# Expert weights of a mixture-of-experts block in twelve 16 KB slots, one 2 MB load each, and no normed copy of the tokens

## The chip, the cores and the metric

The kernel runs on one core of one Trainium2 chip. The metric is the device time in microseconds (us), the median of several runs. All data are float32 in HBM. On the chip, SBUF has 128 partitions; sizes of tiles below are bytes per partition.

## The reference, cut to what matters

256 tokens of width 1024 go through two transformer blocks. Block 1 and the front of block 2 (mixers, attention, a cross attention to a memory) are dense. Behind them stand 16 experts, of which each takes the 32 tokens that score highest for it:

```python
def ec_moe(h, router_w, w_gu, w_down):          # h = rmsnorm(x) * g
    cap = 2 * n // 16                           # 32
    aff = softmax(einsum('bnd,de->bne', h, router_w))
    gates, idx = top_k(swapaxes(aff, 1, 2), cap)
    xs = h[idx]
    def expert(xe, wgu, wd):                    # wgu 1024 x 4096, wd 2048 x 1024
        ga, up = split(xe @ wgu, 2)
        return (silu(ga) * up) @ wd
    ys = map(expert, (xs, w_gu, w_down)) * gates
    return zeros(n, d).at[idx].add(ys)
...
x = x + ec_moe(...)
return rmsnorm(x, final_norm_g)
```

One expert's weights are 16 MB (gate and up) and 8 MB (down); all of them are 384 MB, each byte read once and used for 32 tokens.

## The kernel before

One class, `Body`, writes the program; `run` (L213) calls `block1_mix`, `block1_ffn`, `block2_mix`, `cross` and `moe` one after the other. All loads are issued by the sync engine's queue (SP), in program order: a load that waits for its place holds up those behind it.

**Dense part.** A weight unit of 1 MB is loaded into one of three `raw` buffers (L49, L55), and `split` (L59) turns it into an exact sum of two float32r tiles, `wh` by ScalarE (L67) and `wl` by VectorE (L68). Both come from the ring `hl` of eight 8 KB buffers, so four units are split at a time. `mm3` (L81) multiplies in three passes: H with H, L with H, H with L. `raw` and `hl` lie in one pool, `big`.

**End of the dense part.** `proj_out` with `w_out_2` (L714) multiplies the mixers' output `yH`, `yL` (tiles of the pool `m2`) with four split units. `cross` (L984) then projects queries with two split units of `ca_wq`, from the tokens `xh`, `xl` (pool `xt`, 16 KB), attends to keys and values `mK`, `mV` (pool `mkv`, 8 KB; last read on L1019), and multiplies with `ca_wo` as it is, from two `raw` buffers (L1031). Its small tiles `q`, `qT`, `aE`, `apT` are in the pool `caw`. `route` (L1035) makes the router's logits from `xf`, the transposed tokens (L1054), and has GpSimd write `h`, the tokens times their 1/rms (L1055).

**Experts.** `moe` (L1057) finds each expert's 32 tokens as a one-hot matrix `OH` (L1116). For four experts at a time `gather` (L1126) multiplies `h` with `OH` into `xs`. For each expert (L1119), eight blocks k of 128 rows are loaded in two halves, `eload(wgu[...])` (L1148), each 128 rows of 8 KB, and multiplied on four column groups of TensorE at once (L1150). Then Silu (L1164), times U (L1165), four transposes (L1169), a copy `aT` (L1171), eight `down` loads with their matmuls (L1179), a copy `ys` of each half of the columns (L1190 by ScalarE, L1192 by VectorE, both into one tile), and a matmul that scatters it to the tokens (L1194). The last expert's down weights come in pieces of columns (L1229), so that the end of the work is small; behind that stand the final norm and the store (L1248).

**Slots.** A load goes to the next of 21 slots of 8 KB (L1067 to L1070), in the order in which they fall free: nine pools `e0` to `e8`, opened from the right end of SBUF downwards, the eight `hl` buffers, the three `raw` buffers and `xf`. A pool that lies over older tiles waits for those it overlaps:

```python
e_ = [(self.open("e%d" % i, 1, es, "right"), "e", 1) for i in range(9)]
raw, hl = (self.big, "raw", self.NR), (self.big, "hl", self.NH)
slots = (e_[3:6] + [hl] * 4 + [raw] + [hl] * 4 + e_[:3] + e_[6:8] + [raw] * 2 + e_[8:] + [(ep, "xf", 1)])
```

`eload` (L1077) keeps the loads in their order. On the right side lie, from the end downwards, `xt` (16 KB), `mkv` (8 KB), `m2` (49 KB, whose lowest 16 KB are `yH` and `yL`), and below it tiles of the mixers that are done earlier.

Of the kernel before, what the change touches and what calls it, by code (L numbers as in the profile page):

```python
# [26 lines left out]
class Body:  # L27
# [10 lines left out]
    def psum_pool(self, **banks):  # L38
        """the 8 banks of PSUM, dealt out anew"""
# [7 lines left out]
    def unit(self, w, u, c0):  # L47
        """rows 512 u .. 512 u + 511, 512 columns from c0"""
        raw = self.big.tile([128, 4, 512], F32, name="raw", tag="raw", bufs=self.NR)  # L49
        self.nc.sync.dma_start(raw, w.rearrange("(u k p) c -> u p k c", p=128, k=4)[u][:, :, c0:c0 + 512])  # L50
        return raw

    def unit_c(self, w, c0):
        """1024 rows, 256 columns from c0"""
        raw = self.big.tile([128, 8, 256], F32, name="raw", tag="raw", bufs=self.NR)  # L55
# [15 lines left out]
    def queued(self, behind):  # L71
        """issue what follows behind the given instructions of the same engines"""
# [8 lines left out]
    def mm3(self, out, pairs, first=True, last=True):  # L81
        """pairs: ((lhsT H, lhsT L), (rhs H, rhs L)) per 128 of the contraction."""
# [6 lines left out]
    def gemm_T(self, x, ws):  # L89
        """x @ W by 128 tokens: two of [tok 128, 512]"""  # L90
# [7 lines left out]
    def gemm_t(self, x, ws, t):  # L98
        """x @ W for the tokens of half t: [tok 128, 512]"""
# [6 lines left out]
    def gemm_W(self, x, w, tag="acc"):  # L106
        """(x @ W)^T for 256 columns of W: [feature 128, 2 x 256 tok]"""
# [13 lines left out]
    def rstd(self, ss, n, scale, tag="rs", eng=None):  # L121
        """1/sqrt(ss*scale + eps) on [128, n]: a first guess from the exponent, then Newton's iteration"""
# [23 lines left out]
    def sumsq(self, src, junk):  # L146
        """sum of squares over the free axis of the given [128, n] pieces"""
# [9 lines left out]
    def norm_T(self, x, gname):  # L157
        """rmsnorm(x) * g, transposed, as exact sum H + L; the two halves of the tokens one by one"""
# [30 lines left out]
    def post_norm_a(self, t, halves, eng=None):  # L189
        """1/rms of a half of the tokens"""  # L190
# [5 lines left out]
    def post_norm_b(self, halves, g):  # L196
        """times the gain"""
# [6 lines left out]
    def post_norm_c(self, t, y, r):  # L204
        """x[:, t] += y * r"""
# [7 lines left out]
    def run(self):  # L213
# [8 lines left out]
        self.NR, self.NH = 3, 8  # L222
        self.big = self.open("big", 1)
        st = ExitStack()
# [20 lines left out]
        self.close(self.work2, mkv, self.xtp)  # L245
# [1049 lines left out]
```

## Time and profile before

| | |
|---|---|
| median of 3 runs | 1561.36 us (1559.75 to 1562.66) |
| the profiled execution, first to last instruction (span) | 1558.2 us; the median run is 3.2 us longer |
| TensorE busy | 1286.3 us (83%), mean granted clock 0.875 |
| VectorE, ScalarE, GpSimd busy | 417.2, 351.3, 42.9 us |
| read from HBM | 501.05 MB, 322 GB/s over the span |
| loads of expert weights | 376 of 1 MB; 14, 2 and 4 of 512, 256 and 128 KB at the end |

PE is TensorE's matmuls, PEld its weight loads, DVE VectorE, ACT ScalarE, POOL GpSimd; SPq is the sync engine's queue, which issues the DMAs. A float32 matmul stands in the trace as two records. Tile names lose their numbers, and the 8 KB slots are called `eraw`. PEclk is the clock granted to TensorE, as a share of 2.4 GHz. Times in the rows are us from the start of the span.

### The profile page before, as it was taken

The page shows a single profiled execution, that of the slowest core. Times are in us where ns is not written, and L with a number is a line of the kernel's source. Part 1 is how long each engine was busy: PE and PEld are TensorE (multiplying, and loading weights), DVE is VectorE, ACT ScalarE, POOL GpSimd, SP SyncE. Part 2 cuts the span into 40 slices and gives each one's busy share as a digit, 9 for nine tenths or more (in the row PEclk, how much of TensorE's full clock was granted, in tenths as well). Part 3 has the DMA queues.
Part 4 walks back from the last instruction along what each step waited for, and adds up shares of the span by engine and source line. Part 5 has one row for each costly group of instructions (what it writes and reads, how often), then busy time and mean ns, then how long its engine had stood idle before and what let it go on. Part 6 is the DMA issues. An engine that isn't in the chain of part 4 may idle for free.

```text
span 1558.2 us, 17805 instructions
## 1 busy us (share of the span) xinstructions
PE 1286.3 (83%) x7429; PEld 680.1 (44%) x7429; DVE 417.2 (27%) x753; ACT 351.3 (23%) x608; POOL 42.9 (3%) x97
## 2 busy tenths in 40 slices
PE   6999999999999998886777777768767768777676
PEld 5998988999978775321121111112111102111112
DVE  5644557544467764200000000000000000000002
ACT  5445546444356643000000000000000000000002
POOL 1100012000020001000000000000000000000000
PEclk9999999999999999897868868778779778778777
DMA  8744437555532389899999999999999999999996
GB/s 272 242 162 135 156 117 240 191 190 189 180 112 94 110 321 365 346 420 420 421 421 421 420 421 421 420 421 420 421 421 421 420 421 420 421 420 421 421 420 244
DMA packets 137360, 503.26 MB, mean 323 GB/s; under 512 B 14251, under 2 KB 68287, under 8 KB 89152
## 3 DMA queue, kind: packets, MB, share of 16 engines
q1 hardware_dynamic: 137280, 502.13, 82.0%
q8 instruction: 58, 0.95, 0.3%
q14 instruction: 22, 0.18, 0.0%
HBM read 501.05 MB, written 1.05 MB: 322 GB/s over the span
## 4 chain that ended last, share of the span: by engine, by line
DMA 56%; PE 11%; DVE 1%; ACT 1%; issue 0%; SPq 0%; DVEq 0%; ACTq 0%
DMA eraw<-in_expert_w_gu_dram 37%; DMA eraw<-in_expert_w_down_dram 19%; PE acc L86 4%; PE sm L1150 1%; PE acc L1031 1%; PE sm L86 1%; PE sm L1179 1%; PE po L955 0%; PE sm L1132 0%; PE at L947 0%; PE sm L765 0%; PE sm L870 0%; PE po L1019 0%; PE at L978 0%; PE sm L1012 0%
## 5 line engine op out<-in xcount | busy, mean ns | idle before, releaser
L1150 PE MATMUL sm<-eraw,xs 128*32 128x512 f32 x2048 | 366.4, 811 | 168.4 <-DMA eraw<-in_expert_w_gu_dram 168.4
L1179 PE MATMUL sm<-eraw,aT 128*32 128x512 f32 (+2 forms) x1088 | 227.0, 672 | 42.0 <-DMA eraw<-in_expert_w_down_dram 30.6
L1150 PEld LDWEIGHTS sm<-eraw,xs 128*32 128x32 f32 x2048 | 48.9, 123 | 459.5 <-DMA eraw<-in_expert_w_gu_dram 423.1
L68 DVE TENSOR_TENSOR wl<-raw,wh 128x1024 fp32r<-128x1024 f32 x166 | 197.8, 1220 | 101.1 <-ACT wh L67 100.8
L67 ACT ACTIVATE wh<-raw 128x1024 fp32r<-128x1024 f32 x166 | 168.1, 1054 | 154.2 <-PE sm L86 67.7
L1165 DVE TENSOR_TENSOR es<-es,sm 128x512 f32<-128x512 f32 x16 | 11.0, 687 | 570.0 <-PE sm L1150 564.0
L1179 PEld LDWEIGHTS sm<-eraw,aT 128*32 128x32 f32 x1088 | 53.6, 121 | 201.4 <-DMA eraw<-in_expert_w_down_dram 93.0
L1164 ACT ACTIVATE es<-sm 128x512 f32<-128x512 f32 x16 | 9.6, 597 | 444.9 <-PE sm L1150 444.8
L1192 DVE COPY ys<-sm 128x512 f32<-128x512 f32 (+2 forms) x18 | 11.3, 632 | 235.5 <-PE sm L1179 235.5
L1190 ACT ACTIVATE ys<-sm 128x512 f32<-128x512 f32 x16 | 9.6, 597 | 252.3 <-PE sm L1179 252.3
L1194 PE MATMUL acc<-ys,ogT 128*128 128x512 f32 (+2 forms) x136 | 59.8, 581 | 1.3 <-ACT ys L1190 0.8
L86 PE MATMUL acc<-xh,wl 128*128 128x256 f32 x352 | 51.6, 284 | 0.0
L86 PE MATMUL acc<-xl,wh 128*128 128x256 f32 x352 | 50.4, 282 | 0.0
L86 PE MATMUL acc<-xh,wh 128*128 128x256 f32 x352 | 50.0, 283 | 0.0
L86 PE MATMUL sm<-xh,wh 128*128 128x256 f32 x352 | 49.6, 284 | 0.0
L86 PE MATMUL sm<-xh,wl 128*128 128x256 f32 x352 | 48.9, 281 | 0.0
L86 PE MATMUL sm<-xl,wh 128*128 128x256 f32 x352 | 48.9, 281 | 0.0
L86 PEld LDWEIGHTS sm<-xh,wh 128*128 128x128 f32 x352 | 46.1, 191 | 0.6
L86 PEld LDWEIGHTS acc<-xh,wl 128*128 128x128 f32 x352 | 45.5, 189 | 0.5
L86 PEld LDWEIGHTS acc<-xh,wh 128*128 128x128 f32 x352 | 45.0, 188 | 0.5
L86 PEld LDWEIGHTS acc<-xl,wh 128*128 128x128 f32 x352 | 45.2, 189 | 0.1
L86 PEld LDWEIGHTS sm<-xh,wl 128*128 128x128 f32 x352 | 44.9, 189 | 0.0
(381 smaller groups left out, 1337.0 us busy)
## 6 DMA issues: line engine op xcount, KB each, us to landing
eraw<-in_expert_w_gu_dram SPq DMA_DIRECT2D x256, 1024.0 KB, 19.8
eraw<-in_expert_w_down_dram SPq DMA_DIRECT2D x120, 1024.0 KB, 19.8
raw<-in_w_in_dram SPq DMA_DIRECT2D x34, 1024.0 KB, 5.2
raw<-in_w_gate_dram SPq DMA_DIRECT2D x11, 1024.0 KB, 5.2
raw<-in_w_up_dram SPq DMA_DIRECT2D x11, 1024.0 KB, 5.2
raw<-in_w_down_dram SPq DMA_DIRECT2D x11, 1024.0 KB, 4.9
raw<-in_w_out_dram SPq DMA_DIRECT2D x8, 1024.0 KB, 4.9
eraw<-in_expert_w_down_dram SPq DMA_DIRECT2D x14, 512.0 KB, 11.6
```

The source lines that it names most:

```text
L67: nc.scalar.activation(H[:, k], raw[:, k], AF.Copy)
L68: self.at["L"] = nc.vector.tensor_tensor(L[:, k], raw[:, k], H[:, k].bitcast(F32), OP.subtract).ins
L86: nc.tensor.matmul(out, l[i], r[j], start=first and p == 0 and q == 0, stop=last and p == 2 and q == n - 1)
L1031: nc.tensor.matmul(acc[c], o[:, k, t * 128:(t + 1) * 128], w[c][:, k, :], start=k == 0, stop=k == 3)
L1150: nc.tensor.matmul(dst[32 * j:32 * j + 32, :], xs[:, k, 32 * q:32 * q + 32], raw[:, 512 * j:512 * j + 512], start=k == 0, stop=k == 7, til ...
L1164: nc.scalar.activation(s, G, AF.Silu)
L1165: nc.vector.tensor_tensor(s, s, U, OP.mult)
L1179: nc.tensor.matmul(y[c0][32 * c:32 * c + 32, 0:n], aT[:, c, 32 * j:32 * j + 32], raws[hh][:, o:o + n], start=j == 0, stop=j == 3, tile_pos ...
L1190: nc.scalar.activation(ys[:, c], y[c0][:, 0:n], AF.Copy)
L1192: nc.vector.tensor_copy(ys[:, c], y[c0][:, 0:n])
L1194: nc.tensor.matmul(out[t], ogT[:, t * 128:(t + 1) * 128], ys[:, c], start=first, stop=last)
```

## The change

- The two halves of a split unit become one 16 KB tile; `hl` is a ring of four. `raw` gets a pool of its own, `rawp`, closed ahead of `moe`. `ep` is opened at the start.
- The slots are twelve of 16 KB: eight pools from the right end, and the four `hl` buffers. `raw` and `xf` are slots no more; `xf` moves to `cross`'s pool `ca`.
- One load brings 2 MB: a block of 128 whole rows of the gate and up weights (16 KB each), or 512 rows of down weights, four to a partition (16 KB in one run).
- `h` is gone: `gather` multiplies `x`. Each expert gets the 1/rms of its 32 tokens by eight matmuls of one column (`OH` with `rc`), a copy `rs`, and applies it as the scale of Silu and in the multiplication with U.
- `ys` is a tile of one half of the columns, in one buffer of 2 KB. The final norm's row, its copies and the junk tile share one slot.
- The scratch memory for descriptors of GpSimd's DMAs falls to 1 KB per partition; the kernel issues none.

```diff
-        raw = self.big.tile([128, 4, 512], F32, name="raw", tag="raw", bufs=self.NR)
+        raw = self.rawp.tile([128, 4, 512], F32, name="raw", tag="raw", bufs=self.NR)
...
-        H = self.big.tile([128, n, c], F32R, name="wh", tag="hl", bufs=self.NH)
-        L = self.big.tile([128, n, c], F32R, name="wl", tag="hl", bufs=self.NH)
+        HL = self.big.tile([128, 2, n, c], F32R, name="whl", tag="hl", bufs=self.NH)
+        H, L = HL[:, 0], HL[:, 1]
...
-        self.NR, self.NH = 3, 8
+        self.NR, self.NH = 3, 4
+        self.ep = self.open("ep", 1)
         self.big = self.open("big", 1)
+        rawst = ExitStack()
+        self.rawp = self.open("rawp", 1, rawst)
...
-        self.close(self.work2, mkv, self.xtp)
+        self.close(rawst, mkv, self.xtp)
...
-            self.h = self.sb(self.ep, [128, 2, D], "h4")
-            self.xf = self.sb(rt, [128, 8, 256], "xf", tag="xf")
+            self.xf = self.sb(ca, [128, 8, 256], "xf")
+            self.rc = self.sb(rt, [128, 2], "rc")
...
-        ss = self.sumsq([x[:, t, 0:512], x[:, t, 512:1024]], h[:, t, :])
+        ss = self.sumsq([x[:, t, 0:512], x[:, t, 512:1024]], cw.tile([128, 512], F32, name="sqj", tag="q"))
...
+        nc.gpsimd.tensor_copy(self.rc[:, t:t + 1], self.r4[t])
...
-        nc.gpsimd.tensor_scalar(h[:, t, :], x[:, t, :], self.r4[t], None, OP.mult)
...
-            e_ = [(self.open("e%d" % i, 1, es, "right"), "e", 1) for i in range(9)]
-            raw, hl = (self.big, "raw", self.NR), (self.big, "hl", self.NH)
-            slots = (e_[3:6] + [hl] * 4 + [raw] + [hl] * 4 + e_[:3] + e_[6:8] + [raw] * 2 + e_[8:] + [(ep, "xf", 1)])
+            e_ = [(self.open("e%d" % i, 1, es, "right"), "e", 1) for i in range(8)]
+            hl = (self.big, "hl", self.NH)
+            slots = e_[2:5] + [hl] * 2 + e_[:1] + [hl] * 2 + e_[1:2] + e_[5:8]
...
-                return pool.tile([128, 2048], F32, name="eraw", tag=tag, bufs=bufs)
+                return pool.tile([128, 4096], F32, name="eraw", tag=tag, bufs=bufs)
...
-                    for half, dst in ((0, G), (1, U)):
-                        raw = eload(wgu[e, 128 * k:128 * k + 128, 2048 * half:2048 * half + 2048])
+                    raw = eload(wgu[e, 128 * k:128 * k + 128, :])
+                    for o, dst in ((0, G), (2048, U)):
...
                 p = self.ps()
+                for j in range(4):
+                    for t in range(2):
+                        nc.tensor.matmul(p[32 * j:32 * j + 32, 256:257], OH[:, t, e, :], self.rc[:, t:t + 1],
+                                         start=t == 0, stop=t == 1, tile_position=(0, 32 * j))
+                rs = self.small.tile([128, 1], F32, name="rsl", tag="st9", bufs=2)
+                nc.vector.tensor_copy(rs, p[:, 256:257])
...
-                nc.scalar.activation(s, G, AF.Silu)
-                nc.vector.tensor_tensor(s, s, U, OP.mult)
+                nc.scalar.activation(s, G, AF.Silu, scale=rs)
+                nc.vector.scalar_tensor_tensor(s, U, rs, s, OP.mult, OP.mult)
...
-                def rows(j, hh):
-                    return wdn[e, 512 * j + 256 * hh:512 * j + 256 * hh + 256].rearrange("(p i) n -> p i n", i=2)
-
-                ys = ew.tile([128, D], F32, name="ys", tag="ys")
+                def rows(j):
+                    return wdn[e, 512 * j:512 * j + 512].rearrange("(p i) n -> p i n", i=4)
...
                 def scatter(c0, n, out, first, last):
-                    c = slice(c0, c0 + n)
+                    ys = ew.tile([128, n], F32, name="ys", tag="ys")
...
-                        raws = [eload(rows(j, hh).rearrange("p i n -> p (i n)")) for hh in range(2)]
+                        raw = eload(rows(j).rearrange("p i n -> p (i n)"))
...
-                        for hh in range(2):
-                            nc.sync.dma_start(raws[j][hh].rearrange("p (i n) -> p i n", i=2)[:, :, c0:c0 + m],
-                                              rows(j, hh)[:, :, c0:c0 + m])
+                        nc.sync.dma_start(raws[j].rearrange("p (i n) -> p i n", i=4)[:, :, c0:c0 + m],
+                                          rows(j)[:, :, c0:c0 + m])
...
-    nc = bacc.Bacc("TRN2", target_bir_lowering=False, num_devices=1)
+    nc = bacc.Bacc("TRN2", target_bir_lowering=False, num_devices=1, dynamic_dma_scratch_size=1024)
```

## Rows read from the trace of the kernel before

**Rows 1.** Chain that ended last, in order of time: start, us, what.
```profile
654.40 8.29 PE sm L1179 x53
662.69 20.07 DMA eraw<-in_expert_w_gu_dram
...
1534.94 9.48 DMA eraw<-in_expert_w_down_dram
```

**Rows 2.** Windows: us, busy us of each engine, PEclk, DMA share, GB/s.
```profile
100.00:200.00 100.00, 99.43 (x698) 89.83 (x697) 53.38 (x93) 54.09 (x99) 0.00 (x0) 1.00 0.46 153
...
565.50:602.50 37.00, 36.04 (x171) 26.18 (x170) 19.93 (x51) 16.06 (x40) 0.00 (x0) 1.00 1.01 413
602.50:607.50 5.00, 4.96 (x32) 3.61 (x31) 4.10 (x14) 2.68 (x7) 0.00 (x0) 1.00 0.27 102
...
626.00:633.00 7.00, 6.07 (x32) 3.20 (x32) 2.58 (x11) 0.00 (x0) 0.00 (x0) 0.61 0.10 27
...
640.00:1520.00 880.00, 655.92 (x3248) 143.29 (x3248) 34.82 (x58) 34.28 (x62) 0.00 (x0) 0.80 1.01 421
```

**Rows 3.** Waits of the SP queue, 640 to 1500: us in total, times, longest.
```profile
SPq L1080 <- DMA eraw<-in_expert_w_gu_dram: 482.5, 229, 3.4
```

**Rows 4.** DMA issues, whole span: KB each, median us from issue to landing.
```profile
eraw<-in_expert_w_gu_dram SPq DMA_DIRECT2D x256, 1024.0 KB, 19.8
```

**Rows 5.** SP queue in order of time, windows of 1 us: start, us, line, tiles.
```profile
564.79 1.55 SPq L1080 DMA_DIRECT2D eraw<-in_expert_w_gu_dram  x3
...
591.85 1.28 SPq L1080 DMA_DIRECT2D eraw<-in_expert_w_gu_dram  x3
...
606.46 0.81 SPq L1080 DMA_DIRECT2D eraw<-in_expert_w_gu_dram  x2
...
618.50 0.33 SPq L1080 DMA_DIRECT2D eraw<-in_expert_w_down_dram  x1
631.59 0.33 SPq L1080 DMA_DIRECT2D eraw<-in_expert_w_down_dram  x1
```

**Rows 6.** TensorE in order of time, 569 to 634: start, us, line, tiles.
```profile
573.77 0.39 PE L86 MATMUL sm<-wl,yH 128*128 128x512 f32 x1
...
605.27 1.16 PE L1019 MATMUL po<-apT,mV 128*128 128x128 f32 x8
...
616.46 1.96 PE L1054 MATMUL po<-rw,xf 128*128 128x16 f32 x16
...
629.60 2.82 PE L1150 MATMUL sm<-eraw,xs 128*32 128x512 f32 x16
```

**Rows 7.** DMA queue in 640:1500, 283.7:288.5, 295.4:300.4: packets, MB, share of 16 engines.
```profile
q1 hardware_dynamic: 49622, 361.34, 101.1%
...
q1 hardware_dynamic: 1040, 1.05, 64.1%
...
q1 hardware_dynamic: 272, 1.05, 60.2%
```

**Rows 8.** TensorE in order of time, one expert, idle before and its releaser in brackets.
```profile
1399.97 1.94 PE L1150 MATMUL sm<-eraw,xs 128*32 128x512 f32 x8 [1.42 <-DMA eraw<-in_expert_w_gu_dram]
...
1405.28 1.13 PE L1169 MATMUL sm<-ident,es 128*128 128x128 f32 x4 [0.88 <-DVE es L1165]
1407.15 7.50 PE L1179 MATMUL sm<-eraw,aT 128*32 128x512 f32 x32 [0.75 <-ACT aT L1171]
...
1424.22 3.70 PE L1194 MATMUL acc<-ys,ogT 128*128 128x512 f32 x8
```

**Rows 9.** Waits of TensorE and of ScalarE, 0 to 565: us in total, times, longest.
```profile
PE sm L185 <- POOL rstd L129: 10.8, 1, 10.8
...
ACT wh L67 <- PE sm L86: 67.7, 21, 8.0
```

**Rows 10.** TensorE in order of time, end of the last expert.
```profile
1523.46 1.06 PE L1150 MATMUL sm<-eraw,xs 128*32 128x512 f32 x8 [0.80 <-DMA eraw<-in_expert_w_gu_dram]
...
1543.04 2.24 PE L1179 MATMUL sm<-eraw,aT 128*32 128x256 f32 x22 [0.29 <-DMA eraw<-in_expert_w_down_dram]
1545.62 1.13 PE L1194 MATMUL acc<-ys,ogT 128*128 128x256 f32 x4 [0.34 <-DVE ys L1192]
```

More of the change, by code (lines that the diff above doesn't have):

```diff
@@ L53, in unit_c @@
     def unit_c(self, w, c0):
-        raw = self.big.tile([128, 8, 256], F32, name="raw", tag="raw", bufs=self.NR)
+        raw = self.rawp.tile([128, 8, 256], F32, name="raw", tag="raw", bufs=self.NR)
         self.nc.sync.dma_start(raw, w.rearrange("(k p) c -> p k c", p=128)[:, :, c0:c0 + 256])
@@ L506, in mem_T @@
         L = self.sb(pool, [128, 8, 256], "memL", F32R, tag=tags[1])
-        m = self.big.tile([128, 2, D], F32, name="mem", tag="raw", bufs=self.NR)
+        m = self.rawp.tile([128, 2, D], F32, name="mem", tag="raw", bufs=self.NR)
         nc.sync.dma_start(m, self.a["mem_2"][0].rearrange("(t p) d -> p t d", p=128))
@@ L550, in d_unit @@
             def d_unit(j):
-                raw = self.big.tile([128, 4, 512], F32, name="raw", tag="raw", bufs=self.NR)
+                raw = self.rawp.tile([128, 4, 512], F32, name="raw", tag="raw", bufs=self.NR)
                 nc.sync.dma_start(raw.rearrange("p (k h) c -> p k (h c)", k=2),
@@ L601, in unit_kv @@
     def unit_kv(self, u):
-        raw = self.big.tile([128, 4, 512], F32, name="raw", tag="raw", bufs=self.NR)
+        raw = self.rawp.tile([128, 4, 512], F32, name="raw", tag="raw", bufs=self.NR)
         wr = self.a["w_in_2"][0].rearrange("(u k p) c -> u p k c", p=128, k=4)[u]
@@ L699, in block2_mix @@
                 nc.scalar.activation(so[:, t, :], acc[:, 256:512], AF.Tanh, scale=0.5)
-            band = self.big.tile([128, 2, 4, 136], F32, name="band", tag="raw", bufs=self.NR)
+            band = self.rawp.tile([128, 2, 4, 136], F32, name="band", tag="raw", bufs=self.NR)
             nc.sync.dma_start(band, a["band_c"])
@@ L708, in block2_mix @@
             self.close(ms)
-            self.ep = self.open("ep", 1)
-            self.work2 = ExitStack()
-            self.work = self.open("work2", 2, self.work2)
-            self.gains = self.open("gains2", 1, self.work2)
+            work2 = ExitStack()
+            self.work = self.open("work2", 2, work2)
+            self.gains = self.open("gains2", 1, work2)
             xT, factor, scale, trans = self.norm_T(self.x, "norm_mem_g_2")
@@ L716, in block2_mix @@
             self.behind = [(), (p["h", 0], p["s", 0])]
+            self.close(work2)
         return xT
@@ L905, in attn2_rope @@
         kT = self.sb(m2, [128, 256], "kT2")
-        buf = self.big.tile([128, 2048], F32, name="rope", tag="raw", bufs=self.NR)
+        buf = self.rawp.tile([128, 2048], F32, name="rope", tag="raw", bufs=self.NR)
         ro = buf[:, 0:1280].rearrange("p (t h e) -> p t h e", t=2, h=10)
@@ L1098, in moe @@
                 nc.tensor.transpose(p[0:NE, t * 128:(t + 1) * 128], aff[:, t, :], self.ident)
-            tk = ew.tile([NE, 4, 256], F32, name="tk", tag="ys")
+            tk = ew.tile([NE, 4, 256], F32, name="tk", tag="xs")
             w1, w2, mk, po = (tk[:, i, :] for i in range(4))
@@ L1208, in moe @@
                     nc.vector.tensor_tensor(x[:, t, c], x[:, t, c], acc[2 * t + n], OP.add)
-            grow = slot()[0:1, 0:D]
+            end = slot()
+            grow, g, junk = end[0:1, 0:D], end[:, D:2 * D], end[:, 2 * D:3 * D]
             nc.sync.dma_start(grow, a["final_norm_g_2"].rearrange("(o d) -> o d", o=1))
-            g = slot()[:, 0:D]
             for n in range(2):
@@ L1215, in moe @@
                 nc.scalar.activation(g[:, 512 * n:512 * n + 512], p, AF.Copy)
-            junk, fo = slot(), slot().rearrange("p (t n) -> p t n", t=2)
+            fo = slot()[:, 0:2 * D].rearrange("p (t n) -> p t n", t=2)
             ss = self.small.tile([128, 16], F32, name="ss", tag="st1", bufs=4)
@@ L1224, in moe @@
                     if i == 0:
-                        raws[j] = [slot() for _ in range(2)]
+                        raws[j] = slot()
                     m = 512 if j < 3 else n
                     if c0 < 768 or j == 3:
-                        for hh in range(2):
-                            nc.sync.dma_start(raws[j][hh].rearrange("p (i n) -> p i n", i=2)[:, :, c0:c0 + m],
-                                              rows(j, hh)[:, :, c0:c0 + m])
+                        nc.sync.dma_start(raws[j].rearrange("p (i n) -> p i n", i=4)[:, :, c0:c0 + m],
+                                          rows(j)[:, :, c0:c0 + m])
                         if j < 3:
```

31 lines of the change are left out of this document (14 added, 17 removed).

## The prediction, made before the changed kernel was built

> **What bounds the kernel now.** I read the chain of waits first. From 662.69 us to 1544.4 us it is expert loads and, but for short pieces, nothing else; ahead of that it is mostly TensorE [rows 1]. The windows by stage say the same: in the dense part TensorE is busy 99.43 of 100 us at full clock with the DMA engines at 0.46; from 640 to 1520 us the DMA share is 1.01 at 421 GB/s, while TensorE is busy 656 of 880 us [rows 2]. So there are two regimes, and what counts is when the second begins, how fast it runs, and what follows its last byte.
>
> The waits of the SP queue say what holds a load back in the second regime: another load's landing, 482.5 us in 229 waits [rows 3]. A load takes 19.8 us to land [rows 4], and at 421 GB/s 1 MB takes 2.49 us, so eight are always under way. Slots don't limit there.
>
> They do between the regimes. The windows show the DMA engines busy from 565.5 to 602.5, at 0.27 from 602.5 to 607.5, and at 0.10 from 626 to 633 [rows 2]: 0.73 x 5 + 0.90 x 7 = 10 us idle. The first gap is a wait for a slot: three loads go at 591.85, the next at 606.46 [rows 5], behind the attention matmuls that end at 606.4 [rows 6]. In the second all 21 slots are full, and the next load, at 631.59 [rows 5], needs a slot that the first expert has used; its matmuls begin at 629.60 [rows 6], when the router is done.
>
> **The change part by part.** The sum is made against the span of 1558.2 us; the median run is 3.2 us above it.
>
> *A, room ahead of the experts.* 12 slots of 2 MB hold 24 MB, 21 of 1 MB hold 21. If all of it lands before TensorE frees a slot, 3 MB more are there when the stream restarts: 3 x 2.49 = 7.5 us. The restart itself comes later, since a slot is free only when both halves of k = 0 are used: the first 16 records end at 632.42 [rows 6], against 631.59 for the load that now needs one half [rows 5]; 0.8 us. A = -6.7.
>
> Does it all land? I place the slots by adding up the pools' sizes from both ends of SBUF. `e2` lies over mixer tiles that are done: issued at 564.8, where the first is now [rows 5]. `e3` and `e4` lie over `yL` and `yH`, last read by a matmul that starts at 573.77 and takes 0.39 [rows 6]; `w_out_2`'s two `hl` pairs fall free with them: 8 MB at about 574.2. `e0` is `xt`, free with `ca_wq`'s pairs at 591.85 [rows 5]: 6 MB. `e1` (`mkv`) and `e5` (over `aE`, `apT`) follow at 606.5, `e6` and `e7` (over `xf` and `raw`) at 618.5, when the logits' matmuls end [rows 6]. At 2.49 us per MB: 2 MB last to about 574, with a gap of some 1 us; 8 MB to 595; 6 to 610; 4 to 620; 4 to 630. The restart is at 633, so 3 us are left. Were the three last slots free 4 us later, nothing would change; were any of it wrong by more, A would fall towards -3. Bounds -7.5 and -3. Removing `h` is worth nothing: GpSimd wrote it beside other work, and `gather` waits for `OH`, not for it.
>
> *B, the size of the packets.* The stream's cost per byte may change, since each run in HBM is 16 KB and not 8. From 640 to 1500 the queue's packets took 101.1% of 16 x 860 us for 361.34 MB: 40.4 us of engine time per MB (1,048,576 bytes), in 144 packets [rows 7]. A single load of 1 KB runs took 64.1% of 16 x 4.8 = 49.2 us in 1040 packets [rows 7]. The line through both is 38.95 us plus 9.9 ns per packet; with 72 packets per MB it gives 39.66, 1.8% less. Against it, a single load of 4 KB runs, 272 packets, took 60.2% of 16 x 5 = 48.2 us [rows 7], hardly less than the 1 KB one, so part of the difference belongs to lone loads and not to packets. The rate counts on the 352 MB between the first 24, which wait for TensorE anyway, and the last expert's 8, whose pieces keep their runs: 352 x 2.49 = 876 us. Bounds: nothing, if a packet is cut at 8 KB or the time goes by bytes, and 1.8%, 15.6 us. I take 13, near the line, because packets back to back are what the stream is made of. B = -13.
>
> The Trainium skill ("DMA: Bandwidth & Descriptors", section Bandwidth) states a fixed cost of about 2 us per DMA beside its bytes, 341 GB/s for 1 MB and 425 for 16 MB; by it each of 176 loads saved would be worth 2 us, 352 in all. The trace disagrees: 1 MB loads in a stream run at 421 GB/s [rows 2], so with eight under way the fixed cost is hidden, and B goes by packets. The same section puts the ceiling at 435 GB/s, which as an estimate would leave 28 us at most.
>
> *C, the end.* TensorE uses the last gate and up load after its landing: now 1.06 us of matmuls [rows 10], then twice that, or 1.94 more at the lower clock, the length of a burst there [rows 8]. In the last expert TensorE hardly waits: 0.29 us for a load at 1543.04 [rows 10], so of a later start all but that arrives at the end. `ys` in one buffer makes the copy of each further piece of columns wait for the scatter before; such a copy holds TensorE for 0.34 us now [rows 10], and there are two short pieces on the path. C = +2, between +1 and +3.
>
> *At nothing.* Per expert, the 1/rms group is 16 records of one column; the logits' 16 narrow records took 1.96 us [rows 6]. Behind it waits Silu, and behind the `ys` copy the second scatter: about 1 us. TensorE has this in the stream (0.25 of it idle [rows 2]); without the cover it is 3 us x 16. In the dense part a pair in `hl` is free only when H and L both are, one pass of `mm3` later, where the weights are the moving side. ScalarE waits 67.7 us there for matmuls to free its buffers, but TensorE has no wait for a split at all; its eight kinds of waits, the largest 10.8 us, are for norms, masks and attention [rows 9]. With three pairs ahead, the delay stays hidden. `raw` has its three buffers as before.
>
> Sum: 1558.2 - 6.7 - 13 + 2 = 1540.5 us of span, 1543.7 as a median run.
>
> **The rivals.** *The packets don't pay.* The stream stays at 421 GB/s: 1558.2 - 6.7 + 2 + 3.2 = 1556.7. The alike costs of lone 1 KB and 4 KB loads speak for it, the line speaks against it.
>
> *The room doesn't pay.* A late slot in the middle of the order holds up all behind it on SP, and the 24 MB aren't there at 633: 1558.2 - 13 + 2 + 3.2 = 1550.4. For it: four steps of the placing must hold. Against it: 3 us of slack.
>
> *TensorE becomes the bound (slower).* Place: the stream, every expert. Loads of 2 MB bring work in bursts half as often, with pauses twice as long: now a burst of 8 records follows 1.42 us of idling and takes 1.94 us [rows 8], where one at full clock takes 1.06 [rows 10]; the granted clock is 0.80 on average, a mix of the levels 1.2 and 2.4 GHz [rows 2]. If all bursts ran at 1.2 GHz, an expert would be 16 x 1.94 + 2 x 7.50 + 3.70 + 2.8 (transposes and the two waits about them) = 52.5 us [rows 8], plus 2 for the 1/rms group, 1 for `ys` and about 1.5 for gather and gates: 57. The load takes 24 x 2.49 = 59.8. It decides from 60 us per expert on; at 62 it would give 15 x 2.2 = 33 us more than the loads, 1558.2 - 6.7 + 2 + 33 + 3.2 = 1590. For it: only 3 us of margin on that count; against it: in the trace the clock rises wherever work piles up (1.00 in the dense part [rows 2]).
>
> The Trainium skill ("TensorE: Matmul & The Clock Gate", section HAM oscillation) says of waits for DMA between bursts that each next burst starts cold. The trace agrees where 1.42 us of idling are followed by 1.94 us bursts [rows 8], and by the rule this rival gets its chance.
>
> **How the numbers follow.** A measurement of this kernel tells about 0.2%, 3 us, from no change. Forecast (A and B pay): 0.60, own range 1539 to 1551 (B from -15.6 to -8, A to -5, C from +1 to +3). Packets don't pay: 0.24, of which 0.04 ends within 0.2% if A comes short or C long. Room doesn't pay: 0.08. TensorE bound: 0.05. A late pair that does reach TensorE in the dense part: 0.03, slower. So faster 0.88, same 0.04, slower 0.08. The range is 1537 to 1559: the first three cases with their bounds.
>
> **What would show it.** A: a row of 12 issues ending at about 619, no gap near 605, one of 3 to 4 us before 633. B: 427 GB/s in the stream, packets of 16 KB, half as many; 2 MB every 4.91 us. If it stays at 4.98, B is wrong; if packets are 8 KB, for that reason. C: 35 to 37 us from the last gate and up landing to the end, 34.7 now. At nothing: the first expert's matmuls still begin at about 630, and TensorE waits for loads throughout the stream. The prediction is wrong altogether if the matmuls of the experts begin some us later, or SP's waits name matmuls in the stream.

## The result, and the profile after

The changed kernel takes 1548.12 us (median of 4 runs, 1544.64 to 1550.03), against 1561.57 before: the ratio is 0.9914, 95% interval 0.99 to 0.9928. That is 13.4 us faster; forecast were 1543.7 us, with a range of 1537 to 1559.

The two profiled executions split into three parts at two marks, the first matmul of the first expert and the first matmul on the last gate and up load:

| | before | after | difference |
|---|---|---|---|
| start to first expert matmul | 629.60 | 637.73 | +8.1 |
| from there to the last gate and up load | 893.86 | 874.69 | -19.2 |
| from there to the end | 34.7 | 35.9 | +1.2 |
| span | 1558.2 | 1548.3 | -9.9 |

The two marks of the changed kernel (those of the kernel before are in [rows 6] and [rows 10]):

```profile
637.73 3.64 PE L1153 MATMUL sm<-eraw,xs 128*32 128x512 f32 x16
...
1512.42 3.56 PE L1153 MATMUL sm<-eraw,xs 128*32 128x512 f32 x16 [2.99 <-DMA eraw<-in_expert_w_gu_dram]
```

The profiled execution of the changed kernel is its slowest of four (spans 1542.9 to 1548.3); the time of an execution is 1.7 us above its span. If the last two parts hold for all, the medians (-13.4) leave +4.6 us for the first. So the stream gave what was forecast (A and B: -19.7), and the dense part, which was forecast to stay as it was, gave some of it back.

Windows of the changed kernel (columns as in [rows 2]), and two of the kernel before:

```profile
255.00:280.00 25.00, 22.03 (x171) 21.02 (x171) 10.27 (x13) 6.89 (x9) 0.00 (x0) 0.93 0.53 178
576.00:602.50 26.50, 25.75 (x131) 19.66 (x129) 16.35 (x43) 12.45 (x30) 0.00 (x0) 1.00 0.97 400
602.50:607.50 5.00, 4.79 (x18) 2.55 (x17) 1.64 (x5) 1.33 (x6) 0.00 (x0) 1.00 1.02 433
633.00:640.00 7.00, 5.04 (x22) 2.74 (x26) 3.61 (x13) 0.00 (x0) 0.00 (x0) 0.50 0.77 321
640.00:650.00 10.00, 10.00 (x76) 3.80 (x72) 1.03 (x4) 0.00 (x0) 0.00 (x0) 0.90 0.77 292
700.00:1500.00 800.00, 518.71 (x3128) 129.58 (x3124) 33.99 (x64) 30.43 (x54) 0.00 (x0) 0.82 1.01 427
```

```profile
700.00:1500.00 800.00, 591.84 (x2848) 127.18 (x2848) 31.03 (x50) 29.25 (x54) 0.00 (x0) 0.79 1.01 421
255.00:280.00 25.00, 25.00 (x192) 24.07 (x191) 16.51 (x17) 12.48 (x14) 0.00 (x0) 1.00 0.79 256
```

The gap near 605 us [rows 2] is gone. Before the restart 0.23 x 7 + 0.23 x 10 = 3.9 us stay idle, at 633 to 650. The stream runs at 427 GB/s where it ran at 421. Between 255 and 280 us TensorE, busy throughout before, idles 3 of 25 us.

SP's queue of the changed kernel in order of time (as [rows 5]), its waits from 640 to 1500 us (as [rows 3]), a load's landing (as [rows 4]) and the DMA queue there (as [rows 7]):

```profile
573.58 0.34 SPq L1083 DMA_DIRECT2D eraw<-in_expert_w_gu_dram  x1
582.14 2.21 SPq L1083 DMA_DIRECT2D eraw<-in_expert_w_gu_dram  x4
600.02 1.28 SPq L1083 DMA_DIRECT2D eraw<-in_expert_w_gu_dram  x3
614.62 0.81 SPq L1083 DMA_DIRECT2D eraw<-in_expert_w_down_dram  x2
626.66 0.80 SPq L1083 DMA_DIRECT2D eraw<-in_expert_w_down_dram  x2
641.43 0.33 SPq L1083 DMA_DIRECT2D eraw<-in_expert_w_gu_dram  x1
...
SPq L1083 <- DMA eraw<-in_expert_w_gu_dram: 470.5, 104, 6.0
SPq L1083 <- DMA eraw<-in_expert_w_down_dram: 253.3, 56, 6.0
...
eraw<-in_expert_w_gu_dram SPq DMA_DIRECT2D x128, 2048.0 KB, 39.1
...
q1 hardware_dynamic: 25090, 365.59, 100.2%
```

The first twelve expert loads go in the groups 1, 4, 3, 2, 2 that the prediction placed, each 8 to 9 us later than it said. Packets per MB are half of before's. SP waits for landings, 724 of 860 us; TensorE is not the bound.

### The profile page after: what moved, and what is told of

It is laid out like the page before. It is cut to its first block, busy times and chain, and to the rows that moved or that the text cites. A ratio compares the mean times of both kernels' runs of the same rounds, so it can differ in the third digit from the quotient of the medians.

```text
span 1548.3 us, 17883 instructions
## 1 busy us (share of the span) xinstructions
PE 1202.1 (78%) x7685; PEld 684.1 (44%) x7685; DVE 421.3 (27%) x769; ACT 352.3 (23%) x608; POOL 37.4 (2%) x97
## 4 chain that ended last, share of the span: by engine, by line
DMA 54%; PE 2%; SPq 2%; DVE 1%; ACT 0%; issue 0%; DVEq 0%
DMA eraw<-in_expert_w_gu_dram 36%; DMA eraw<-in_expert_w_down_dram 18%; SPq L1233 2%; PE sm L1153 1%; PE sm L1186 1%; PE sm L1135 0%; PE acc L1200 0%; DVE tk L1108 0%; DVE m L1107 0%; DVE OH L1119 0%; ACT L1173 0%; DVE x L1242 0%; PE sm L1177 0%; DVE ys L1198 0%; DVE es L1174 0%
## 5 line engine op out<-in xcount | busy, mean ns | idle before, releaser
L1186 PE MATMUL sm<-eraw,aT 128*32 128x512 f32 (+2 forms) x1088 | 169.1, 758 | 81.6 <-DMA eraw<-in_expert_w_down_dram 73.4
L68 DVE TENSOR_TENSOR whl<-raw,whl 128x1024 fp32r<-128x1024 f32 x166 | 198.0, 1220 | 107.7 <-ACT whl L67 107.6
L67 ACT ACTIVATE whl<-raw 128x1024 fp32r<-128x1024 f32 x166 | 168.2, 1052 | 91.5 <-issue 49.7
L86 PE MATMUL acc<-xh,whl 128*128 128x256 f32 x704 | 95.8, 286 | 0.0
L86 PE MATMUL sm<-xh,whl 128*128 128x256 f32 x704 | 91.7, 283 | 0.0
L86 PEld LDWEIGHTS acc<-xh,whl 128*128 128x128 f32 x704 | 88.8, 191 | 0.8
L86 PEld LDWEIGHTS sm<-xh,whl 128*128 128x128 f32 x704 | 88.2, 191 | 0.6
L86 PE MATMUL acc<-whl,xh 128*128 128x512 f32 x256 | 70.5, 408 | 0.2
L86 PE MATMUL acc<-whl,aH 128*128 128x512 f32 x176 | 57.9, 403 | 2.4 <-ACT aH L118 2.4
L86 PE MATMUL acc<-xl,whl 128*128 128x256 f32 x352 | 51.0, 283 | 0.0
## 6 DMA issues: line engine op xcount, KB each, us to landing
eraw<-in_expert_w_gu_dram SPq DMA_DIRECT2D x128, 2048.0 KB, 39.1
eraw<-in_expert_w_down_dram SPq DMA_DIRECT2D x60, 2048.0 KB, 39.1
```

Source lines behind the costliest of these rows:

```text
L67: nc.scalar.activation(H[:, k], raw[:, k], AF.Copy)
L68: self.at["L"] = nc.vector.tensor_tensor(L[:, k], raw[:, k], H[:, k].bitcast(F32), OP.subtract).ins
L86: nc.tensor.matmul(out, l[i], r[j], start=first and p == 0 and q == 0, stop=last and p == 2 and q == n - 1)
L1186: nc.tensor.matmul(y[c0][32 * c:32 * c + 32, 0:n], aT[:, c, 32 * j:32 * j + 32], raw[:, o:o + n], start=j == 0, stop=j == 3, tile_position ...
```

## The experiments: what made the dense part longer

Around 255 to 280 us, in the changed kernel: SP's queue, VectorE, ScalarE and TensorE (idle before and releaser in brackets), and the rate of the DMA engines in 40 slices of 253 to 275 us.

```profile
254.04 0.43 SPq L639 DMA_DIRECT2D g<-in_q_norm_g_dram  x1
256.26 0.38 SPq L56 DMA_DIRECT2D raw<-in_w_gate_dram  x1
272.41 0.43 DVE L665 TENSOR_SCALAR g<-g 128x512 f32<-128x512 f32 x1 [13.70 <-DMA g<-in_q_norm_g_dram]
275.49 1.06 ACT L67 ACTIVATE whl<-raw 128x1024 fp32r<-128x1024 f32 x1 [15.23 <-DMA raw<-in_w_gate_dram]
277.12 0.79 PE L86 MATMUL acc<-whl,aH 128*128 128x512 f32 x1 [2.42 <-ACT aH L118]
278.46 0.79 PE L86 MATMUL acc<-whl,aL 128*128 128x512 f32 x1 [0.55 <-DVE aL L119]
GB/s 0 104 52 261 432 395 454 341 229 25 19 21 20 21 18 21 18 7 20 15 21 17 21 19 34 55 54 44 60 56 33 57 178 304 363 385 382 346 322 307
```

Block 2's eleven small parameter loads (L631 to L649; two of the expectations below count twelve), which the kernel before issues after block 1's weights, stand here among them. q_norm's in the kernel before:

```profile
426.66 0.42 SPq L636 DMA_DIRECT2D g<-in_q_norm_g_dram  x1
```

In the changed kernel VectorE waits 13.70 us for q_norm's gain, the next weights land 19 us after their issue, and TensorE waits for activations and restarts at half clock (0.79 for a matmul that takes 0.39). Three causes fit: VectorE's wait, with the splits (L68) behind it; the many small loads on SP; or q_norm's load itself, 256 KB in packets of 256 bytes, all read from the same 256 bytes of HBM, during which the engines move some 20 GB/s. And there is the pair that the prediction named.

**Scalings late.**

```diff
-            nc.vector.tensor_scalar(mng, mng, 0.5, None, OP.mult)
-            nc.vector.tensor_scalar(g640[:, 0:8, :], g640[:, 0:8, :], 0.125, None, OP.mult)
+            with self.queued([self.at["x", 1]]):
+                nc.vector.tensor_scalar(mng, mng, 0.5, None, OP.mult)
+                nc.vector.tensor_scalar(g640[:, 0:8, :], g640[:, 0:8, :], 0.125, None, OP.mult)
```

> The changed kernel with one edit: VectorE's two scalings of block 2's parameters (mng by 0.5, g640 by 0.125) are put behind the last addition to x of block 1 on VectorE; the small loads stay where they are. In the changed kernel VectorE waits 13.70 us for the load of q_norm's gain at 258.7 to 272.4 us, and the dense part loses 6 us to the kernel before between 255 and 286 us. Theory 1 (the wait of VectorE for that load, with the splits queued behind it): the three waits of TensorE for aH, aL and the half-clock stretch at 277 to 283 us go, the first expert matmul begins at 631 to 632.5 us instead of 637.73, and the time falls by 5 to 6.5 us, from 1548.1 to about 1542. Theory 2 (a pair of H and L that is freed one pass later): nothing goes, first expert matmul at 637 to 638, 1548 us. Theory 3 (the small loads on SP's queue ahead of the weights' loads): they stand where they stood, so 1546 to 1548 us.

1547.51 us (ratio to before 0.9909, 0.9895 to 0.9922): my first theory fell. VectorE no longer waits there, but the weights come as late as they did, and ScalarE and TensorE wait for them. The trace is of the fastest of four executions (1545.27 us). Its first expert matmul is at 633.24, which is 4.5 us earlier than in the changed kernel's trace; but traces without the edit are as early (the table at the end of this section):

```profile
273.66 1.06 ACT L67 ACTIVATE whl<-raw 128x1024 fp32r<-128x1024 f32 x1 [14.78 <-DMA raw<-in_w_gate_dram]
...
275.29 0.50 PE L86 MATMUL acc<-whl,aH 128*128 128x512 f32 x1 [1.97 <-ACT aH L118]
```

**Loads late too.** With the scalings late as above, the eleven loads are queued behind block 1's last `w_down` (the lines from `gb` to `psc` move in by one level):

```diff
+                self.at["wd"] = nc.sync.dma_start(raw.rearrange("p (k h) c -> p k (h c)", k=2),
...
+            with self.queued([self.at["wd"]]):
```

> As the run with the scalings late, and block 2's twelve small parameter loads are also queued on SP behind the last load of w_down of block 1. Theory 1 (VectorE's wait): the same time as with the scalings late alone, 1542, within 1.5 us. Theory 2 (pairs): 1548. Theory 3 (the small loads hold up SP's queue, which spent 249 to 283 us among them): all of the 6 us come back only here, 1542, while the run with the scalings alone late stays near 1547.

1544.03 us (0.989, 0.9875 to 0.9905). The step between 255 and 286 us is gone from its trace, and the first expert matmul begins at 632.37. So it is the loads, by their number or by q_norm's.

**Gains once.**

```diff
-                nc.sync.dma_start(g640[:, h0:h0 + n, :],
-                                    bass.AP(tensor=g1.tensor, offset=g1.offset, ap=[[0, 128], [0, n], [1, 64]]))
+                nc.sync.dma_start(g640[:, h0:h0 + 1, :],
+                                    bass.AP(tensor=g1.tensor, offset=g1.offset, ap=[[0, 128], [0, 1], [1, 64]]))
...
-            nc.vector.tensor_scalar(g640[:, 0:8, :], g640[:, 0:8, :], 0.125, None, OP.mult)
+            nc.vector.tensor_scalar(g640[:, 0, :], g640[:, 0, :], 0.125, None, OP.mult)
+            nc.vector.tensor_copy(g640[:, 1:8, :], g640[:, 0:1, :].to_broadcast([128, 7, 64]))
+            nc.vector.tensor_copy(g640[:, 9, :], g640[:, 8, :])
```

> The changed kernel with one edit: the gains of q_norm and k_norm are loaded once per partition (64 numbers, 32 KB each over 128 partitions) instead of eight and two times (256 and 64 KB), and VectorE copies them to the heads. All of block 2's small loads stay in their early place. Theory 4, from the two runs with late parameters: what costs the time is not VectorE's wait but q_norm's load itself, 256 KB in packets of 256 bytes that move at about 21 GB/s for some 12 us (262 to 272 us), while the 1 MB of w_gate behind it in the same queue lands 18 to 20 us after its issue; then the step of 6 us between 255 and 286 us falls to 0 to 2, the first expert matmul begins at 631 to 633, and the time is about 1543. Theory 1 (VectorE's wait, whatever it waits for): the same. Theory 3 (the number of small loads on SP's queue, each some 0.4 us to issue): no change, 1547 to 1548.

1543.07 us (0.9888, 0.9874 to 0.9903), 5.0 less than the changed kernel. All eleven loads are as many as in the changed kernel, and as early or earlier (q_norm's is issued at 253.23 us). ScalarE no longer waits for the weights, and from 262 to 272.4 us the engines move 269 GB/s, where the changed kernel moves 78:

```profile
263.55 1.06 ACT L67 ACTIVATE whl<-raw 128x1024 fp32r<-128x1024 f32 x1 [3.14 <-PE sm L86]
...
262.00:272.40 10.40, 10.40 (x90) 10.40 (x89) 5.38 (x7) 5.02 (x6) 0.00 (x0) 1.00 0.81 269
```

The load of q_norm's gain is the cause; k_norm's, which the edit makes smaller too, is issued at 275.56 in the changed kernel, after the wait. Whether q_norm's load is slow for its small packets or for reading one place again and again, no run separates. The same edit in the kernel before:

> The kernel before the change with the one edit of the gains of q_norm and k_norm loaded once per partition. There q_norm's load stands behind block 1's weights, and the shift of 6 us between 255 and 286 us does not exist. If the load costs its time only where the change has moved it, ahead of weights that TensorE is about to need: the same time as before, within 1.5 us of 1561.3. If it costs some 5 us wherever it stands: 1556.

1561.35 us against 1561.71 (1.0, 0.9991 to 1.0009): there the load costs nothing. So the loss comes from its place, and its place from the memory layout. The order of issue in two programs that were built, not run, shows the second: the kernel before with nothing but the last line of the diff (scratch memory of 1 KB, which moves the left pools down by 15,360 bytes) has the eleven loads early, and the changed kernel with 4,000 bytes left free below `m1` has them late. What decides is whether block 1's pool `f1w` reaches over `m2`'s `yH`, which begins at byte 154,496 of a partition: `f1w` ends at byte 161,600 in the kernel before and at 151,360 in the changed one, and at 146,240 and 155,360 in the two built programs. While the two overlap, `m2` must wait for block 1 to end, and the loads into it with it.

**H and L apart.** `hl` is a ring of eight 8 KB tiles again; four 16 KB pools over its memory are the slots.

```diff
-        HL = self.big.tile([128, 2, n, c], F32R, name="whl", tag="hl", bufs=self.NH)
-        H, L = HL[:, 0], HL[:, 1]
+        H = self.big.tile([128, n, c], F32R, name="wh", tag="hl", bufs=self.NH)
+        L = self.big.tile([128, n, c], F32R, name="wl", tag="hl", bufs=self.NH)
...
+            h_ = [(self.open("h%d" % i, 1, es), "e", 1) for i in range(4)]
...
-            slots = e_[2:5] + [hl] * 2 + e_[:1] + [hl] * 2 + e_[1:2] + e_[5:8]
+            slots = e_[2:5] + h_[:2] + e_[:1] + h_[2:] + e_[1:2] + e_[5:8]
```

> The changed kernel with H and L of a split unit as two tiles of 8 KB in a ring of eight again, as before the change; the pool of that ring is closed ahead of the experts, and four pools of 16 KB over the same memory take its place as slots. Block 2's parameters stay early. Theory 1 (VectorE's wait for q_norm's gain): no change, first expert matmul within 1.5 us of 637.73, 1548 us within 2. Theory 2 (the pair): the dense part is as before the change, first expert matmul at 629.5 to 631, 1541 us. A mixed outcome, in which the pair makes the 1.9 us between 540 and 564 us: 635.8 and 1546.

1548.45 us (0.9916, 0.9903 to 0.993): no gain in time. In its trace the step at 255 to 286 us stays, and the dense part's further 1.9 us between 540 and 564 us are gone: its first expert matmul is at 635.32. So the pair costs 1.9 us there, where matmuls of the attention and of the memory's values change places; TensorE stays busy, and its idle time there differs by 0.15 us. But a slot is late instead (SP waits 15.5 us for matmuls into `acc`). With both edits (and the order `h_[2:]`, then `h_[:2]`):

> The changed kernel with two edits together: the gains of q_norm and k_norm once per partition, and H and L as two tiles of 8 KB (ring of eight, four 16 KB pools over its memory as slots; the two that lie over w_out's units come first in the order now). Theory 4 and the mixed outcome of the run with H and L apart: the first takes away the step between 255 and 286 us, the second the 1.9 us between 540 and 564 us, so the first expert matmul begins at 629.5 to 631 and the time is 1541 (1543.07 with the first edit alone). Rival (the 1.9 us are the order of the matmuls, which falls out by chance in each kernel): no less than 1543.

1545.2 us (0.9894, 0.9881 to 0.9908). The first expert matmul is at 630.57, as forecast, yet the time is 2.1 us above that with the gains alone, as the rival had it, though for another reason: a load in the middle of the order waits for a slot, and the engines idle in a stretch where the run with the gains alone has a share of 1.01:

```profile
585.00:595.00 10.00, 9.98 (x56) 7.72 (x55) 2.96 (x10) 4.38 (x13) 0.00 (x0) 1.00 0.33 103
...
SPq L1086 <- PE acc L86: 14.4, 1, 14.4
```

From its first expert matmul to the last gate and up load it takes 877.6 us, 2.9 more than the changed kernel and 2.7 more than the run with the gains alone.

**The traces side by side.** All of them issue the same dense work. Stretch 1 goes from the last matmul of `memL` (near 245 us) to block 1's last matmul of `aH` (near 440), stretch 2 from the last matmul of `v` with `AT` to the last of `yL` in `acc` (some 530 to 570). The last column holds scatter from ahead of 245 us as well, where these traces differ by up to 3.3 us.

| run | q_norm's load | H and L | stretch 1, us | stretch 2, us | first expert matmul |
|---|---|---|---|---|---|
| before | late | apart | 191.6 | 39.2 | 629.60 |
| before, gains once | late, small | apart | 192.5 | 39.3 | 630.24 |
| both edits | early, small | apart | 192.6 | 39.3 | 630.57 |
| both edits, ys twice | early, small | apart | 193.0 | 39.3 | 632.39 |
| gains once | early, small | pair | 193.2 | 41.1 | 631.96 |
| loads late too | late | pair | 193.4 | 41.1 | 632.37 |
| 4 KB runs | early | pair | 194.9 | 41.1 | 632.49 |
| scalings late | early | pair | 195.2 | 41.1 | 633.24 |
| no 1/rms | early | pair | 195.4 | 40.8 | 633.76 |
| H and L apart | early | apart | 197.2 | 39.3 | 635.32 |
| ten slots | early | pair | 197.6 | 41.1 | 636.65 |
| two loads | early | pair | 197.9 | 41.1 | 637.71 |
| changed | early | pair | 198.1 | 41.1 | 637.73 |

The 1.9 us go with the pair in every trace, so they are not chance. The early load costs 2 us in three traces and 4 to 5 in the four others, against gains once. The programs of 4 KB runs, no 1/rms, ten slots, two loads and the changed kernel have the same dense part as built, instruction by instruction. What differs is the clock with which TensorE restarts after the pause: at 280 to 285 us it is granted 0.64 in the changed kernel and 1.00 without 1/rms, after much the same waits, so part of the 5.0 us is the clock after the pause and not the pause itself. The changed kernel, then the run without 1/rms:

```profile
280.00:285.00 5.00, 5.00 (x16) 3.98 (x15) 5.00 (x6) 3.25 (x4) 0.00 (x0) 0.64 0.83 257
```

```profile
276.35 0.50 PE L86 MATMUL acc<-whl,aH 128*128 128x512 f32 x1 [2.13 <-ACT aH L118]
...
280.00:285.00 5.00, 5.00 (x32) 4.45 (x31) 4.54 (x5) 2.54 (x3) 0.00 (x0) 1.00 0.88 268
```

## The experiments: room, packets, the end, 1/rms

**Ten slots.**

```diff
-            slots = e_[2:5] + [hl] * 2 + e_[:1] + [hl] * 2 + e_[1:2] + e_[5:8]
+            slots = e_[2:5] + [hl] * 2 + e_[:1] + [hl] * 2 + e_[1:2] + e_[5:6]
```

> The changed kernel with ten slots instead of twelve: the last two of the order (over xf and the raw buffers) are left out, so 20 MB instead of 24 can be on chip when TensorE frees the first slot. If the room counts in full, as term A of the prediction has it, 4 MB are missing at the restart of the stream: 4 x 2.45 us = 9.8 us more, 1558, and the DMA engines stand idle for some 10 us more between 618 and 643 us. If half of that memory is not yet landed at the restart anyway, 5 us more, 1553. If the room does not count, 1548.

1557.98 us (0.9974, 0.9963 to 0.9985): +9.9 us for 4 MB, 2.47 us per MB, so the room counts in full. The engines stand still until the restart:

```profile
626.00:633.00 7.00, 0.38 (x1) 0.09 (x1) 5.59 (x20) 0.46 (x2) 0.18 (x1) 0.58 0.17 70
633.00:640.00 7.00, 6.12 (x26) 2.74 (x26) 2.58 (x12) 0.00 (x0) 0.00 (x0) 0.50 0.00 0
```

**Two loads of 1 MB per slot, runs of 8 KB.**

```diff
-                    e_last[:] = [nc.sync.dma_start(raw, src).ins]
+                    for c in (slice(0, 2048), slice(2048, 4096)):
+                        e_last[:] = [nc.sync.dma_start(raw[:, c], src[:, c]).ins]
```

> The changed kernel with each 2 MB slot filled by two loads of 1 MB, the left and the right half of its columns, in runs of 8 KB, as before the change; slots, matmuls and order stay. Theory (the size of the packets or of the loads sets the rate; term B): the stream goes back from 427 to 421 GB/s, so 352 MB take 12 to 13 us more: 1560 to 1561. Rival (the rate comes from something else, such as the slots being freed in larger steps, or TensorE's bursts): 427 GB/s stay, 1548.

1561.53 us (1.0002, 0.9992 to 1.0012): the gain of the change is gone.

**Loads of 2 MB in runs of 8 KB.** The matmuls, the transposes and the down loads follow the new tiles.

```diff
-                    raw = eload(wgu[e, 128 * k:128 * k + 128, :])
+                    b, half = k // 2 * 2, k % 2
+                    raw = eload(wgu[e, 128 * b:128 * b + 256, 2048 * half:2048 * half + 2048].rearrange("(k p) n -> p k n", p=128),
+                                lambda r: r.rearrange("p (k n) -> p k n", k=2))
...
```

> The changed kernel with loads of 2 MB as it has them, but in runs of 8 KB: a load brings the gate halves of two blocks of 128 rows, the next one the up halves of the same two, and a down load two runs of 8 KB per partition. So the size of the load is the new one and that of the packets the old one. Theory (packets): 421 GB/s, 1560. Rival (size or number of loads): 427 GB/s, 1548.

1560.83 us (0.9998, 0.9988 to 1.0007), the median of eleven executions. One of them, the profiled one, took 3695.74 us, so there is no trace of this run to read; the median of the other ten is 1560.30 us.

**Loads of 1 MB in runs of 4 KB.** A tile holds the same halves of two blocks, in quarters; the matmuls, the transposes and the down loads follow suit.

```diff
+                    raw = eload(wgu[e, 128 * b:128 * b + 256, 2048 * half:2048 * half + 2048].rearrange("(k p) (c n) -> c p k n", p=128, c=2),
+                                lambda r: r.rearrange("p (c k n) -> c p k n", c=2, k=2))
...
+                    for c in range(2):
+                        e_last[:] = [nc.sync.dma_start(view(raw)[c], src[c]).ins]
...
```

> The changed kernel with each slot filled by two loads of 1 MB in runs of 4 KB. By the line of the prediction, 9.9 ns of a DMA engine per packet: 288 packets per MB instead of 72 cost 216 x 9.9 = 2.1 us of 16 engines' time per MB, 0.13 us per MB, so 400 to 405 GB/s and 352 x 0.13 = 47 us more: 1595. If the cost per packet between 8 and 16 KB (427 against 421 GB/s, 72 packets per MB less: 0.57 us of engine time, 7.9 ns each) holds on: 407 GB/s, 1586. If runs of 4 KB cost no more than those of 8 KB: 421 GB/s, 1560.

1586.15 us (1.0165, 1.0143 to 1.0186), the second of the three forecasts. Large loads with the old runs are as slow as small ones with the old runs: the run decides, not the load. The DMA queue from 640 to 1500 us in runs of 8 KB (two loads) and of 4 KB, with the stream's window:

```profile
q1 hardware_dynamic: 49377, 359.63, 100.8%
...
700.00:1500.00 800.00, 593.83 (x3092) 132.29 (x3084) 34.00 (x64) 30.43 (x54) 0.00 (x0) 0.83 1.01 420
```

```profile
q1 hardware_dynamic: 91139, 351.35, 102.3%
...
700.00:1500.00 800.00, 583.64 (x2974) 144.91 (x2972) 30.51 (x58) 29.44 (x52) 0.00 (x0) 0.94 1.03 409
```

With 16 x 860 us, the changed kernel's 100.2% for 365.59 million bytes in 25090 packets are 37.71 us of engine time and 68.6 packets per million bytes; here 38.57 us and 137.3, and 40.06 us and 259.4. The slopes are 0.86 / 68.7 = 12.5 ns and 1.49 / 122.1 = 12.2 ns per packet: one line through all three. These times add up to more than the 16 engines have (100.8 and 102.3%), and the more so the shorter the runs, so the stream loses less than they say. By its rates of 427, 420 and 409 GB/s, a million bytes take 37.5, 38.1 and 39.1 us of 16 engines, which makes some 9 and 8 ns per packet: near the 7.9 ns of the forecast that came true.

**ys twice at the end**, on top of gains once with H and L apart.

```diff
-                    ys = ew.tile([128, n], F32, name="ys", tag="ys")
+                    ys = ew.tile([128, n], F32, name="ys", tag="ys2" if n < 512 and c0 != 768 else "ys")
```

> The run with both edits (gains once, H and L apart), and ys of the last expert's second and fourth piece of columns in a buffer of its own (1 KB), so that a copy need not wait for the scatter before. Term C of the prediction put the whole end at 2 us more, of which the two short waits are the part that this takes back: if they are, the end from the last gate and up burst falls from 35.7 to 35, and the time by 0.5 us against the run with both edits. If the waits are only the copy's own time, nothing changes.

1543.65 us (0.9886, 0.9872 to 0.9899), 1.6 less than without, with ranges that overlap (1542.9 to 1545.5 against 1544.34 to 1546.06). The end takes 33.7 us instead of 35.4. TensorE's waits for the copies of VectorE there fall from 1.1 to 0.4 us, without and with the second buffer:

```profile
PE acc L1203 <- DVE ys L1201: 1.1, 3, 0.6
```

```profile
PE acc L1203 <- DVE ys L1201: 0.4, 1, 0.4
```

So 0.7 us are the buffer's, as was expected. The other 1.0 are not accounted for by it. One source of such differences is the clock: after the last landing TensorE is at half clock in the changed kernel and at full clock in the run with late loads, whose `ys` is unchanged. The same scatter of 256 columns, changed kernel and then that run:

```profile
1534.53 1.97 PE L1200 MATMUL acc<-ys,ogT 128*128 128x256 f32 x4
```

```profile
1528.15 1.13 PE L1202 MATMUL acc<-ys,ogT 128*128 128x256 f32 x4
```

**No 1/rms.** The eight matmuls and `rs` go as well.

```diff
-                nc.scalar.activation(s, G, AF.Silu, scale=rs)
-                nc.vector.scalar_tensor_tensor(s, U, rs, s, OP.mult, OP.mult)
+                nc.scalar.activation(s, G, AF.Silu)
+                nc.vector.tensor_tensor(s, s, U, OP.mult)
```

> The changed kernel without each expert's 1/rms: the eight matmuls of one column, the copy rs and both uses of it are left out, so the experts' inputs are not normed. The prediction put this work at nothing, hidden behind the loads of the stream, and at 3 us x 16 = 48 us if the cover were gone. Hidden: 1548, stream still at 427 GB/s, and at most 0.5 us at the end. Not hidden: down to 1500. Partly (only where the last expert and the first burst stand): 1545 to 1547.

1543.05 us (0.988, 0.9867 to 0.9894), 5.1 less than the changed kernel. In its trace the stream is 3.0 us shorter (871.73 from the first expert matmul to the last gate and up load):

```profile
q1 hardware_dynamic: 25366, 368.26, 100.5%
```

That is 37.55 us of engine time per million bytes, 0.4% below 37.71, at nearly the same number of packets (68.9 per million bytes against 68.6). Leaving `rs` out has also moved the four left slots by 64 bytes, to multiples of 256. The Trainium skill ("DMA: Bandwidth & Descriptors", How a descriptor splits into AXI transactions) says that a transaction must start at a multiple of 256 bytes, and that a descriptor that starts elsewhere fetches bytes that it does not use. It says so of reads; these slots are written, and no run here keeps 1/rms and moves the slots. Whether its work or the slots' place costs the 3 us stays open. The rest of the 5.1 is not its work in the dense part, which is the same in both programs: their traces reach the first expert matmul at 633.76 and 637.73 mostly for the clock after the pause, as shown above.

## Why the prediction was right, and which step failed

The time lies in the range, and even in the forecast's own range of 1539 to 1551 us. But A, B and C add up to nearly what they did (-17.7 forecast, -18.0 in the profiled pair), and what separates 1548.12 from 1543.7 is in none of the terms. That the own range was wide enough for it is luck. The prediction named this sign itself: it would be "wrong altogether if the matmuls of the experts begin some us later", and they begin 8.1 us later in the profiled pair. Its sums for A, B and C stand all the same; the part on the dense work does not.

**What bounds the kernel:** right. Two regimes, and in the second SP waits for landings.

**A:** right. The twelve expert loads, their order and the idle 3.9 us are those that were forecast, and 2.47 us per MB stands where 2.49 was used. A and B together were to give -19.7 and gave -19.2 between the two marks.

**B:** right, by its own mechanism: with runs of 8 KB, 13.4 us of the gain are lost with small loads and 12.2 (without the long execution) with large ones. The line through the old stream and one lone load gave 9.9 ns per packet; streams give 8 to 9 by their rates. The rate rose by 1.4% (421 to 427 GB/s), 352 x 2.49 x 0.014 = 12.3 us where 13 were taken and the line said 15.6. The other lone load, which spoke against the line, was no guide to a stream. The Trainium skill states a fixed cost of some 2 us per DMA ("DMA: Bandwidth & Descriptors", section Latency and other measured facts). It does not show here: half as many loads with the same runs gained 1.2 us in all (1560.30 against 1561.53), within the scatter.

**C:** +2 forecast, +1.2 in the profiled pair, at the low bound; over the traces of kernels with the same end it is -0.2 to +1.2 (34.5 to 35.9 us). `ys` has its part, 0.7 us; TensorE's clock at the last landing moves the end as much.

**At nothing:** this step failed. It costed the dense part by the ring of pairs and by `raw` alone; the lines about pools and scratch memory were counted as room and not as order. They moved eleven small loads ahead of block 1's weights, one of them slow: 5.0 us between the medians; in the traces, 2 us where TensorE restarts at full clock behind it and 4 to 5 where it does not. No line of the diff names the loads that it moved. The late pair, given 0.03 as a rival, is there as well, with 1.9 us, not in the form that was priced (TensorE waiting for a split), but in the order of the matmuls. With the one load made small, the kernel takes 1543.07 us against the 1543.7 forecast, with the pair still costing its 1.9 us, so a part of that closeness is chance. The 1/rms work, also put at nothing, is open.

**Rivals.** Packets that don't pay and room that doesn't pay are out; the second one's mechanism, one late slot that holds up those behind it, is what cost 2.7 us with both edits. TensorE as the bound is out: it is busy 519 of 800 us in the stream where it was 592. Not every burst after a wait ran at the lower clock, as that rival took it: 16 records took 1.92 us in some and some 3.6 us in others. What is left are waits for loads of 256 of 860 us (640 to 1500 us, total, times, longest):

```profile
PE sm L1153 <- DMA eraw<-in_expert_w_gu_dram: 184.3, 90, 3.7
PE sm L1186 <- DMA eraw<-in_expert_w_down_dram: 71.4, 40, 4.3
```

**The base.** The 3.2 us between span and median were 1.7 around an execution and 1.5 because the profiled execution of before is one of the short ones; the sum was the same.

## What to carry to other kernels

A change of memory layout is a change of order: pools that no longer overlap free loads that used to wait, and these go ahead of work that is due sooner; compare the order of issue of both programs before costing anything at nothing. A stream that keeps the DMA engines full is made faster by longer runs, here by some 8 to 9 ns of one engine per packet saved, and not by fewer loads. Room ahead of such a stream is worth its transfer time, as long as the engines would otherwise stand still, and one late slot in a fixed order spends it.

## What was not expected of the hardware

- A load of 256 KB that reads one run of 256 bytes 1024 times kept the engines at some 20 GB/s, and 1 MB behind it in the same queue landed 19 us after its issue, against a median of 5.3 for such loads in the changed kernel. Ahead of work with slack, the same load cost nothing.
- Executions of one kernel differ by 5 us (spans 1542.9 to 1548.3). The traces show one source: bursts after a pause run at either clock. The same dense program restarts at 0.64 or at 1.00 behind q_norm's load, which is worth 2 to 3 us; 16 matmul records take 3.64 us at the first expert and 1.92 at others; the last scatters take 1.97 or 1.13. That this also separates executions of one kernel is likely but not shown, since each kernel has one trace.
